# A hybrid attention and recurrence layer: merge-gate projections change places between two stages, and a hand-written timetable is redrawn

## The chip, the core and the metric

The kernel runs on one core of one Trainium2 chip. The metric is device time in microseconds (us) of one execution. The core's engines are PE (TensorE, matrix multiplication into PSUM banks), DVE (VectorE), ACT (ScalarE), POOL (GpSimd) and SP (SyncE, which issues the DMA transfers here). Each works through its own queue in order and waits for the others by semaphores.

## The reference

One decoder layer over 1024 tokens of width 1024. Two branches are computed from the same normalized input and merged by gates:

```python
xn = rms_norm(x, norm_g)
z = xn @ w_in                    # q, c_kv, q_idx, k_idx, w_idx, g_attn, x_rnn, g_rnn, merge
o = sparse_mla_attention(...)    # 16 heads; each query attends to the 256 keys with the best index scores
y_attn = (o * silu(g_attn)) @ w_attn_proj
h = rg_lru(causal_depthwise_conv(x_rnn, conv_w, conv_b), ...)   # gates r, i; a linear scan over time
y_rnn = (h * silu(g_rnn)) @ w_rnn_proj
gates = sigmoid(merge + b_merge)
g_a, g_r = gates[..., :1024], gates[..., 1024:]
return x + (g_a * y_attn + g_r * y_rnn) @ w_out       # and a final rms_norm
```

So there are two sets of merge gates: g_a (in the kernel "ma", for attention) and g_r ("mr", for the recurrence). Both are projections of the normalized input, and neither is needed before its branch's result.

## The kernel before

All activations are held transposed, channels on the 128 partitions and 1024 tokens along the free axis, so each projection of width 1024 is 8 tiles of 128 channels. A value is split into a high and a low fp32r part, and a product takes three matmuls (hi x hi, hi x lo, lo x hi). One projection tile is two halves of 512 tokens, 8 k-steps each, 48 matmuls (`proj_steps`, L115). Its weights come by DMA in two halves (`load_w`, L105): ACT makes the high part, POOL subtracts to get the low part (`split`, L93 to L95). The pool of weight parts holds two tiles, so weights are fetched one tile ahead.

The stages in order:

1. Normalization, the indexer's scores and two ma tiles (0 and 1) beside them.
2. The recurrence stage, written as a timetable: `at_time(t, fn, ...)` (L449) puts calls on a list `plan` with a time in planned us; the list is sorted and run (L822), and that order is then kept on PE, ACT, DVE and POOL (L821). SP's order is left to the scheduler. Planned times only order the work; each engine starts an instruction as soon as its inputs are there.
   - `long(t, kind, c)` (L515) places one projection tile in 16 steps of 0.68. Kinds: "xr" (recurrence input), "gr" (its SiLU gate), "ma", "mr", "rp" (recurrence output projection, which reads the recurrence's result u). A list `amid` of gate parts can be placed between the steps.
   - Four pairs of channel tiles. In each: one filling tile (ma), two xr, two gr. `conv` (L551) convolves on DVE; `both_parts` (L559) splits the result in two halves (ACT and POOL, tiles xs); `gate_part` (L567) makes the recurrence's gates on PE; `tail` (L743) places decay, root and scan of the pair one pair later; `scan` (L602) writes u to DRAM (u_r).
   - Beside this the threshold search for the 256 best keys, bit by bit, 31 rounds: `near_round` (L665) for four blocks of queries on DVE, `far_round` (L674) for the two longest on ACT with a small step on DVE.
   - The tail of the stage (from L783): another ma, eight mr and eight rp tiles on PE. `reload` (L738) fetches u from DRAM into two buffers in turn and splits it for rp. When a search ends, `needs` (L707) and `select` (L715) write each block's mask of distances `sd`; the last addition of `select` is on POOL (L728). `evac_rp` (L507) multiplies y_rnn by the gate mr on DVE and stores it (mr_d).
3. Attention: a planner (`step`, `work`, L1116 to L1154) puts projections for the next pair of heads (q, k, v, g) between the logits, transposes and outputs of the present pair; only PE's order is fixed. `left`, L1157, and L1165 put one merge tile, ma7, beside head pair 6. `merge` (L876) computes it and stores it (ga_d). `gated` (L1012) multiplies a finished pair's o by its gate and stores it.
4. Output projections of attention, merging, the final projection, normalization.

Of the kernel before, what the change touches and what calls it, by code (L numbers as in the profile page):

```python
# [8 lines left out]
F32 = mybir.dt.float32  # L9
# [43 lines left out]
def hybrid_kernel(ctx: ExitStack, tc: tile.TileContext, x, w_b, w_a, w_ap, w_rp, w_o, vecs,  # L53
# [36 lines left out]
    ga_d = [tc.dram_tile([P, S], F32, name=f"ga_d{c}") for c in range(8)]  # L90
    mr_d = [tc.dram_tile([P, S], F32, name=f"mr_d{c}") for c in range(8)]
# [59 lines left out]
    with ExitStack() as p12:  # L151
# [317 lines left out]
        def weights_of(kind, c):  # L469
            src = w_rp[c] if kind == "rp" else w_b[{"xr": G_XR, "gr": G_GR, "ma": G_MA, "mr": G_MR}[kind] + c]  # L470
            W[kind, c] = load_w(src, f"{kind}{c}")
# [20 lines left out]
        def evac_ma(n):  # L492
            g = (here["rn"] if "rn" in here else later["kp2"]).tile([P, S], F32, tag="ga", name=f"ga{n}", bufs=1)

            def evac(c0, m, acc):
                nc.scalar.activation(g[:, c0:c0 + m], acc, AF.Tanh, scale=0.5, bias=hbm[:, n:n + 1])
                nc.sync.dma_start(ga_d[n][:, c0:c0 + m], g[:, c0:c0 + m])
            return evac

        def evac_mr(n):  # L500
            g = gr[n] = grp.tile([P, S], F32, tag="gr", name=f"grm{n}")

            def evac(c0, m, acc):
                nc.scalar.activation(g[:, c0:c0 + m], acc, AF.Sigmoid, bias=col(V_BM + 8, n))
            return evac

# [8 lines left out]
        def long(t, kind, c, amid=(), first=5):  # L515
# [4 lines left out]
            evac = {"xr": evac_xr, "gr": evac_gr, "ma": evac_ma, "mr": evac_mr, "rp": evac_rp}[kind]  # L520
# [194 lines left out]
        def select(b):  # L715
# [12 lines left out]
            nc.gpsimd.tensor_tensor(out=sd[:, off(b):off(b + 1)], in0=s, in1=eq, op=ALU.add)  # L728
# [9 lines left out]
        def reload(c):  # L738
            raw = later["kp2"].tile([P, S], F32, tag=("eq", "pre")[c % 2], name=f"ur{c}")
            nc.sync.dma_start(raw, u_r[c])  # L740
            split(later["uh"][:, c], later["ul"][:, c], raw, nc.gpsimd if c % 3 == 2 else nc.vector)

        def tail(t, c, d):  # L743
            at_time(t + 2.0, decay, c)
            at_time(t + 5.4, radicand, c)
            at_time(t + 6.2, decay, d)
            at_time(t + 12.2, radicand, d)
            at_time(t + 12.3, root, c)
            at_time(t + 12.4, root, d)
            at_time(t + 14.0, scan, c)  # L750
            at_time(t + 20.4, scan, d)
# [3 lines left out]
        t, fill_in = 0.0, iter(range(2, 8))  # L755
        for p in range(4):
            c, d = 2 * p, 2 * p + 1
            t0 = t
            if p:
                tail(t0, c - 2, c - 1)  # L760
                near_round(t0 + 0.8)
                near_round(t0 + 7.0)
            else:
                for u in range(4):
                    near_round(t0 + 3.0 + 5.2 * u)
            at_time(t0 + 1.0, gate_weights, c)
            at_time(t0 + 12.5, gate_weights, d)
# [12 lines left out]
            t = long(t3, "gr", d, gate_parts(d), 3)  # L780
# [9 lines left out]
        at_time(t0 + 27.5, close_rec)  # L790
        at_time(t0 + 27.6, distances)
        near_round(t0 + 27.0)
        for c in range(8):
            at_time(t0 + 32.0 + 1.5 * c, reload, c)
# [618 lines left out]
```

## Time and profile before

| | us |
|---|---|
| median of 3 runs | 1252.97 (1252.04 to 1254.42) |
| the profiled execution | 1251.78 |
| its span, first to last instruction | 1249.9 |
| PE busy in the span | 1160.5 |
| DVE busy | 836.5 |
| ACT busy | 753.1 |
| POOL busy | 472.6 |
| mean granted TensorE clock | 0.967 |

In the profile a matmul's end is modelled and consecutive matmuls overlap, so a busy PE isn't a PE at its peak: the step from one matmul to the next tells more. The granted clock shows when PE was slowed. A line of a group gives the line in the code, the engine, the operation, what it writes and reads, the count, busy time, the mean in ns, and the idle time before it with what ended it. A line of the waits says who waited for whom: us in total, times, longest.

### The profile page before, as it was taken

To read this page: it belongs to the slowest core of one execution; us is meant where nothing else is said; L and a number is where in the kernel's file an instruction comes from. 1 tells how busy PE (TensorE), PEld (TensorE's weight loads), DVE (VectorE), ACT (ScalarE), POOL (GpSimd) and SP (SyncE) were. 2 spreads that over 40 slices of the span, in tenths; PEclk is the share of its full clock that TensorE was granted. 3 is DMA by queue.
4 is the path that set the end of the run, shared out by engine and by line. 5 is a ranking of instruction groups with operands and counts; after the bars stand their busy time and mean duration, and the time that the engine had idled before them with its cause. 6 is when DMAs were issued, how large, how long until landed. Compare 5 with 4: busy or idle time off the path is not lost.

```text
span 1249.9 us, 16199 instructions
## 1 busy us (share of the span) xinstructions
PE 1160.5 (93%) x5528; PEld 964.1 (77%) x5528; DVE 836.5 (67%) x1740; ACT 753.1 (60%) x1444; POOL 472.6 (38%) x385
## 2 busy tenths in 40 slices
PE   6989989999999989969999998988998999999997
PEld 5978868777777768848888776777877877788886
DVE  6887596868696677860387868776867598542335
ACT  6467459696969877311477766666667677332211
POOL 4211135455455322332344352525343526275000
PEclk8989999999999979979999998989999999999999
DMA  5111111222122422112200010110010232264322
GB/s 205 42 34 49 46 55 64 97 72 81 64 83 63 156 87 76 59 51 91 74 12 26 29 34 32 41 33 29 16 38 26 74 112 85 90 202 147 110 85 110
DMA packets 42674, 89.99 MB, mean 72 GB/s; under 512 B 5088, under 2 KB 8672, under 8 KB 42592
## 3 DMA queue, kind: packets, MB, share of 16 engines
q1 hardware_dynamic: 42448, 88.70, 21.2%
q8 instruction: 44, 0.72, 0.2%
q14 instruction: 38, 0.31, 0.1%
q10 hardware_dynamic: 144, 0.26, 0.1%
HBM read 68.49 MB, written 20.45 MB: 71 GB/s over the span
## 4 chain that ended last, share of the span: by engine, by line
PE 64%; DVE 20%; ACT 9%; issue 3%; POOL 1%; DMA 1%; SPq 0%; ACTq 0%; DVEq 0%; POOLq 0%
PE pT L1248 4%; DVE junk L631 3%; PE o L1202 2%; PE z_q L121 2%; PE z_q L122 2%; DVE xc L557 2%; PE f L113 2%; PE f L112 2%; PE f L111 2%; PE z_q L123 2%; PE l L1044 2%; PE l L1045 2%; PE z_ma L122 2%; PE z_ma L123 2%; PE z_ma L121 2%
## 5 line engine op out<-in xcount | busy, mean ns | idle before, releaser
L1251 ACT ACTIVATE pp<-pT 128x512 fp32r<-128x512 f32 (+1 forms) x160 | 87.8, 550 | 55.4 <-PE pT L1248 53.8
L1252 DVE TENSOR_TENSOR pp<-pT,pp 128x512 fp32r<-128x512 f32 (+1 forms) x160 | 100.7, 632 | 28.4 <-ACT pp L1251 26.7
L631 DVE TENSOR_SCALAR_CACHE_REDUCE junk<-sc,thr 128x384 bf16<-128x384 f32 (+4 forms) x130 | 106.3, 817 | 3.5
L1202 PE MATMUL o<-pp,vt 128*128 128x512 f32 x160 | 70.9, 443 | 17.2 <-DVE o L1217 13.8
L654 ACT ACTIVATE junk<-sc,neg 128x896 int8<-128x896 f32 (+1 forms) x62 | 67.8, 1093 | 17.7 <-DVE neg L661 16.6
L1052 ACT ACTIVATE l<-l,m 128x128 f32<-128x128 f32 (+4 forms) x80 | 54.3, 678 | 28.9 <-DVE m L1046 27.7
L1044 PE MATMUL l<-kh,qt 128*128 128x128 f32 (+2 forms) x192 | 66.5, 350 | 2.6 <-DVE m L1046 2.4
L1045 PE MATMUL l<-kl,qt 128*128 128x128 f32 (+2 forms) x192 | 66.9, 349 | 0.0
L121 PE MATMUL z_q<-xh,whi_q 128*128 128x512 f32 x128 | 55.4, 433 | 10.2 <-DVE kl L928 10.2
L123 PE MATMUL z_mr<-xh,wlo_mr 128*128 128x512 f32 x128 | 51.0, 398 | 11.4 <-POOL wlo_mr L95 11.4
L1046 DVE CUSTOM_DVE_ANT_0 l<-sc,l 128x512 f32<-128x512 f16 (+3 forms) x80 | 41.6, 523 | 26.8 <-PE l L1045 24.5
L1052 ACT ACTIVATE sc<-sc,m 128x384 f32<-128x384 f32 (+2 forms) x48 | 44.9, 935 | 23.4 <-DVE m L1046 22.2
L1217 DVE TENSOR_TENSOR o<-o,o 64x256 f32<-64x256 f32 x128 | 52.8, 418 | 8.9 <-ACT o L1215 6.5
L122 PE MATMUL z_rp<-url,whi_rp 128*128 128x512 f32 x128 | 52.4, 410 | 3.3 <-DVE url L95 1.7
L121 PE MATMUL z_rp<-urh,whi_rp 128*128 128x512 f32 x128 | 52.4, 409 | 3.2 <-ACT urh L94 3.1
L95 POOL TENSOR_TENSOR xs<-xc,xs 64x1024 fp32r<-64x1024 f32 x16 | 38.2, 2389 | 43.8 <-ACT xs L94 28.5
L377 ACT ACTIVATE r<-s 128x512 f32<-128x512 f32 (+1 forms) x80 | 39.8, 522 | 25.0 <-PE s L376 22.1
L1248 PE MATMUL pT<-ident,sc 128*128 128x128 f32 x288 | 50.0, 278 | 2.9 <-DVE pp L1252 2.9
L382 DVE SCALAR_TENSOR_TENSOR sc<-r,wi,sc 128x384 f32<-128x384 f32 (+5 forms) x42 | 40.6, 999 | 18.0 <-ACT r L377 17.7
L1057 POOL TENSOR_SCALAR sc<-sc,m 128x384 f32<-128x384 f32 (+1 forms) x32 | 25.6, 801 | 70.5 <-DVE m L1054 57.2
L123 PE MATMUL z_rp<-urh,wlo_rp 128*128 128x512 f32 x128 | 51.9, 405 | 0.0
L1248 PE MATMUL pT<-ident,l 128*128 128x128 f32 x288 | 49.6, 276 | 2.1 <-DVE m L1054 2.1
(358 smaller groups left out, 3928.0 us busy)
## 6 DMA issues: line engine op xcount, KB each, us to landing
xt<-in_x_dram SPq DMA_DIRECT2D x8, 512.0 KB, 8.9
wraw_xr<-in_w_b_dram SPq DMA_DIRECT2D x16, 256.0 KB, 2.7
wraw_gr<-in_w_b_dram SPq DMA_DIRECT2D x16, 256.0 KB, 2.9
u_r<-ig SPq DMA_DIRECT2D x8, 512.0 KB, 2.6
ur<-u_r SPq DMA_DIRECT2D x8, 512.0 KB, 3.3
wraw_mr<-in_w_b_dram SPq DMA_DIRECT2D x16, 256.0 KB, 2.8
wraw_rp<-in_w_rp_dram SPq DMA_DIRECT2D x16, 256.0 KB, 2.9
mr_d<-grm SPq DMA_DIRECT2D x16, 256.0 KB, 2.0
```

The source lines that it names most:

```text
L121: nc.tensor.matmul(acc, wh, xh_, start=(k == 0), stop=False)
L122: nc.tensor.matmul(acc, wh, xl_, start=False, stop=False)
L123: nc.tensor.matmul(acc, wl, xh_, start=False, stop=(k == KT - 1))
L631: nc.vector.tensor_scalar(junk[:, :P * (b + 1)], SL(b), thr_, None, op0=op, op1=ALU.add, accum_out=cnt[:, b - B0:b - B0 + 1])
L654: nc.scalar.activation(junk2[:, :P * (b + 1)], SL(b), AF.Sign, bias=nf[:, j:j + 1], accum_out=sums[:, j:j + 1])
L1044: nc.tensor.matmul(acc[:, :n], q, kh[:, c0:c0 + n], start=True, stop=False)
L1045: nc.tensor.matmul(acc[:, :n], q, kl[:, c0:c0 + n], start=False, stop=True)
L1052: nc.scalar.activation(l[:, :L], l[:, :L], AF.Exp, scale=-1.0, bias=mi, accum_out=m[:, 2:3])
L1202: nc.tensor.matmul(ov, vt[:, 2 * jj, :], pp[:, :, 0:256], start=(jj == 0), stop=False)
L1248: nc.tensor.transpose(tp[:, k * P:(k + 1) * P], pr[u][:, j * P:(j + 1) * P], ident)
L1251: latest[:] = [nc.scalar.activation(pp[:, 0, :n], tp[:, :n], AF.Copy), nc.vector.tensor_tensor(out=pp[:, 1, :n], in0=tp[:, :n], in1=pp[:, ...
L1252: nc.vector.tensor_tensor(out=pp[:, 1, :n], in0=tp[:, :n], in1=pp[:, 0, :n].bitcast(F32), op=ALU.subtract)]
```

## The change

The filling tile of each recurrence pair becomes an mr tile (mr0 to mr3 instead of ma2 to ma5). Their gates are stored to DRAM (gm_d) and fetched again (`again`) when rp has freed buffers; the tail keeps mr4 to mr7 and then runs rp in the order 4 to 7, 0 to 3. The ma tiles 2 to 7 all go to attention, one beside each of the head pairs 1 to 6. u is fetched at once, eight transfers straight into the tile of the low part, and split in place. The addition at the end of `select` gets a place of its own on the timetable. The places of convolutions, decays, roots, scans and search rounds change.

```diff
         def evac_mr(n):
-            g = gr[n] = grp.tile([P, S], F32, tag="gr", name=f"grm{n}")
+            if "rn" in here and n < 4:
+                g = T("g", n, bufs=1)
+            else:
+                g = gr[n] = grp.tile([P, S], F32, tag="gr", name=f"grm{n}")
 
             def evac(c0, m, acc):
                 nc.scalar.activation(g[:, c0:c0 + m], acc, AF.Sigmoid, bias=col(V_BM + 8, n))
+                if n not in gr:
+                    nc.sync.dma_start(gm_d[n][:, c0:c0 + m], g[:, c0:c0 + m])
             return evac
+
+        def again(n):
+            g = gr[n] = grp.tile([P, S], F32, tag="gr", name=f"grm{n}")
+            nc.sync.dma_start(g, gm_d[n])
...
-            nc.gpsimd.tensor_tensor(out=sd[:, off(b):off(b + 1)], in0=s, in1=eq, op=ALU.add)
+            later["sum", b] = lambda: nc.gpsimd.tensor_tensor(out=sd[:, off(b):off(b + 1)], in0=s, in1=eq, op=ALU.add)
+
+        def select_at(t, b):
+            at_time(t, select, b)
+            t += 0.0066 * P * (b + 1) + 0.7
+            at_time(t, lambda: later["sum", b]())
+            return t
...
-        def reload(c):
-            raw = later["kp2"].tile([P, S], F32, tag=("eq", "pre")[c % 2], name=f"ur{c}")
-            nc.sync.dma_start(raw, u_r[c])
-            split(later["uh"][:, c], later["ul"][:, c], raw, nc.gpsimd if c % 3 == 2 else nc.vector)
+        def fetch_u(c):
+            nc.sync.dma_start(later["ul"][:, c].bitcast(F32), u_r[c])
+
+        def part_u(c):
+
+            split(later["uh"][:, c], later["ul"][:, c], later["ul"][:, c].bitcast(F32),
+                  nc.gpsimd if c % 3 == 2 else nc.vector)
 
         def tail(t, c, d):
-            at_time(t + 2.0, decay, c)
-            at_time(t + 5.4, radicand, c)
-            at_time(t + 6.2, decay, d)
-            at_time(t + 12.2, radicand, d)
-            at_time(t + 12.3, root, c)
-            at_time(t + 12.4, root, d)
-            at_time(t + 14.0, scan, c)
-            at_time(t + 20.4, scan, d)
+            for u in (c, d):
+                at_time(t + 2.0, decay, u)
+                at_time(t + 5.36, radicand, u)
+                at_time(t + 5.4, root, u)
+            at_time(t + 12.4, scan, c)
+            at_time(t + 17.5, scan, d)
...
             if p:
                 tail(t0, c - 2, c - 1)
                 near_round(t0 + 0.8)
-                near_round(t0 + 7.0)
-            else:
-                for u in range(4):
-                    near_round(t0 + 3.0 + 5.2 * u)
+                far_round(t0 + 15.0)
...
-            t = long(t, "ma", next(fill_in))
-            far_round(t + 6.1)
-            far_round(t + 12.9)
+            t = long(t, "mr", p)
             t1 = long(t, "xr", c)
             t2 = long(t1, "xr", d)
-            at_time(max(t1 + 1.0, t0 + 26.0), conv, c)
-            at_time(max(t1 + 6.4, t0 + 31.4), both_parts, c)
-            near_round(t0 + 31.5)
-            at_time(t2 + 3.4, conv, d)
-            at_time(t2 + 8.7, both_parts, d)
-            near_round(t2 + 8.8)
-            t3 = long(t2, "gr", c, gate_parts(c))
-            t = long(t3, "gr", d, gate_parts(d), 3)
+            at_time(t1 + 0.8, conv, c)
+            at_time(t1 + 6.0, both_parts, c)
+            near_round(t1 + 6.1)
+            far_round(t1 + 2.4)
+            at_time(t2 + 0.8, conv, d)
+            at_time(t2 + 6.0, both_parts, d)
+            near_round(t2 + 6.1)
+            t3 = long(t2, "gr", c, gate_parts(c), 4)
+            near_round(t3 - 1.4)
+            t = long(t3, "gr", d, gate_parts(d), 4)
+            near_round(t - 7.5)
             far_round(t - 3.4)
 
         t0 = t
         tail(t0, 6, 7)
         near_round(t0 + 0.8)
-        near_round(t0 + 7.0)
-        t = long(t, "ma", next(fill_in))
-        for n in range(3):
+        for n in range(4, 8):
             t = long(t, "mr", n)
...
-            at_time(t0 + 32.0 + 1.5 * c, reload, c)
-        for n in range(8):
+            at_time(t0 + 24.0, fetch_u, c)
+            at_time(t0 + 28.7 + 2.5 * c, part_u, c)
+        for n in (4, 5, 6, 7, 0, 1, 2, 3):
             t = long(t, "rp", n)
-            if n + 3 < 8:
-                t = long(t, "mr", n + 3)
-        u = t0 + 17.0
+            if n > 3:
+                at_time(t + 1.0, again, n - 4)
+        u = t0 + 15.0
         while bits["far"] >= 0:
             far_round(u)
-            u += 5.0
+            u += 4.7
         far_end = u
-        u = t0 + 45.0
+        u = t0 + 23.2
         while bits["near"] >= 0:
-            u = max(near_round(u), u + 5.6)
-        at_time(u, nearest)
+            u = max(near_round(u), u + 5.0)
+        at_time(t0 + 60.0, nearest)
         at_time(u, needs, near, 0, n1)
         u += 4.0
         for b in near:
-            at_time(u, select, b)
-            u += 0.0075 * P * (b + 1)
+            u = select_at(u, b)
         u = max(u, far_end)
         at_time(u, far_last)
         at_time(u + 4.0, needs, FAR_B, n1, nb)
+        u += 7.0
         for b in FAR_B:
-            at_time(u + 7.0, select, b)
+            u = select_at(u, b)
...
-            left = [7]
+            left = list(range(2, 8))
...
-                m = [(i, []) for i in both("m", left.pop(0))] if hp == 6 else []
+                m = [(i, []) for i in both("m", left.pop(0))] if 0 < hp < 7 else []
```

More of the change, by code (lines that the diff above doesn't have):

```diff
@@ L90, in hybrid_kernel @@
     ga_d = [tc.dram_tile([P, S], F32, name=f"ga_d{c}") for c in range(8)]
+    gm_d = [tc.dram_tile([P, S], F32, name=f"gm_d{c}") for c in range(4)]
     mr_d = [tc.dram_tile([P, S], F32, name=f"mr_d{c}") for c in range(8)]
@@ L469, in weights_of @@
         def weights_of(kind, c):
-            src = w_rp[c] if kind == "rp" else w_b[{"xr": G_XR, "gr": G_GR, "ma": G_MA, "mr": G_MR}[kind] + c]
+            src = w_rp[c] if kind == "rp" else w_b[{"xr": G_XR, "gr": G_GR, "mr": G_MR}[kind] + c]
             W[kind, c] = load_w(src, f"{kind}{c}")
@@ L490, in evac_gr @@
             return evac
[L492 to L498, printed above, removed]
         def evac_mr(n):
-            g = gr[n] = grp.tile([P, S], F32, tag="gr", name=f"grm{n}")
+            if "rn" in here and n < 4:
+                g = T("g", n, bufs=1)
+            else:
+                g = gr[n] = grp.tile([P, S], F32, tag="gr", name=f"grm{n}")
             def evac(c0, m, acc):
                 nc.scalar.activation(g[:, c0:c0 + m], acc, AF.Sigmoid, bias=col(V_BM + 8, n))
-            return evac
+                if n not in gr:
+                    nc.sync.dma_start(gm_d[n][:, c0:c0 + m], g[:, c0:c0 + m])
+            return evac
+        def again(n):
+            g = gr[n] = grp.tile([P, S], F32, tag="gr", name=f"grm{n}")
+            nc.sync.dma_start(g, gm_d[n])
         def evac_rp(n):
@@ L519, in long @@
             at_time(begin[order[-2]] + 0.3 if len(order) > 1 else t - LONG, weights_of, kind, c)
-            evac = {"xr": evac_xr, "gr": evac_gr, "ma": evac_ma, "mr": evac_mr, "rp": evac_rp}[kind]
+            evac = {"xr": evac_xr, "gr": evac_gr, "mr": evac_mr, "rp": evac_rp}[kind]
             rhs = (lambda k: (later["uh"][:, k], later["ul"][:, k])) if kind == "rp" else xhl
@@ L736, in close_rec @@
             later["ul"] = urp.tile([P, KT, S], F32R, name="url")
-        def reload(c):
-            raw = later["kp2"].tile([P, S], F32, tag=("eq", "pre")[c % 2], name=f"ur{c}")
-            nc.sync.dma_start(raw, u_r[c])
-            split(later["uh"][:, c], later["ul"][:, c], raw, nc.gpsimd if c % 3 == 2 else nc.vector)
-        def tail(t, c, d):
-            at_time(t + 2.0, decay, c)
-            at_time(t + 5.4, radicand, c)
-            at_time(t + 6.2, decay, d)
-            at_time(t + 12.2, radicand, d)
-            at_time(t + 12.3, root, c)
-            at_time(t + 12.4, root, d)
-            at_time(t + 14.0, scan, c)
-            at_time(t + 20.4, scan, d)
+        def fetch_u(c):
[3 more added lines that the diff above has]
+                  nc.gpsimd if c % 3 == 2 else nc.vector)
+        def tail(t, c, d):
+            for u in (c, d):
[4 more added lines that the diff above has]
+            at_time(t + 17.5, scan, d)
         at_time(-LONG - 1, open_rec)
         at_time(-5.0, signs)
-        t, fill_in = 0.0, iter(range(2, 8))
+        t = 0.0
         for p in range(4):
@@ L785, in hybrid_kernel @@
         near_round(t0 + 0.8)
-        near_round(t0 + 7.0)
-        t = long(t, "ma", next(fill_in))
-        for n in range(3):
+        for n in range(4, 8):
             t = long(t, "mr", n)
-        at_time(t0 + 27.5, close_rec)
-        at_time(t0 + 27.6, distances)
-        near_round(t0 + 27.0)
+        at_time(t0 + 23.0, close_rec)
+        at_time(t0 + 23.1, distances)
         for c in range(8):
-            at_time(t0 + 32.0 + 1.5 * c, reload, c)
-        for n in range(8):
+            at_time(t0 + 24.0, fetch_u, c)
+            at_time(t0 + 28.7 + 2.5 * c, part_u, c)
+        for n in (4, 5, 6, 7, 0, 1, 2, 3):
             t = long(t, "rp", n)
-            if n + 3 < 8:
-                t = long(t, "mr", n + 3)
-        u = t0 + 17.0
+            if n > 3:
+                at_time(t + 1.0, again, n - 4)
+        u = t0 + 15.0
         while bits["far"] >= 0:
             far_round(u)
-            u += 5.0
+            u += 4.7
         far_end = u
-        u = t0 + 45.0
+        u = t0 + 23.2
         while bits["near"] >= 0:
-            u = max(near_round(u), u + 5.6)
-        at_time(u, nearest)
+            u = max(near_round(u), u + 5.0)
+        at_time(t0 + 60.0, nearest)
         at_time(u, needs, near, 0, n1)
```

## The prediction

> **What bounds the kernel now.** I read the page first, then busy time by stage (columns: window, length, then busy us and instruction count of PE, PEld, DVE, ACT and POOL, the granted clock, DMA share, GB/s), then PE's waits inside the two stages that the change touches.
>
> ```profile
> PE 1160.5 (93%) x5528; PEld 964.1 (77%) x5528; DVE 836.5 (67%) x1740; ACT 753.1 (60%) x1444; POOL 472.6 (38%) x385
> ```
> ```profile
> 141.00:389.30 248.30, 236.45 (x1030) 192.85 (x1029) 191.31 (x281) 182.98 (x289) 125.79 (x84) 0.99 0.22 72
> 389.30:432.80 43.50, 43.50 (x193) 36.04 (x192) 29.46 (x46) 36.83 (x63) 15.10 (x12) 1.00 0.37 125
> 432.80:555.00 122.20, 106.23 (x435) 83.16 (x433) 93.42 (x183) 64.97 (x138) 32.97 (x25) 0.92 0.21 69
> 555.00:603.60 48.60, 46.71 (x191) 37.51 (x192) 3.44 (x5) 7.60 (x14) 15.79 (x14) 0.93 0.29 94
> 603.60:618.70 15.10, 15.10 (x80) 12.97 (x78) 7.83 (x13) 8.82 (x17) 6.95 (x7) 1.00 0.20 66
> 618.70:1077.80 459.10, 423.73 (x2207) 352.13 (x2206) 346.33 (x916) 325.67 (x677) 192.61 (x172) 0.96 0.13 42
> ```
> ```profile
> PE rg L573 <- POOL xs L95: 11.9, 7, 5.7
> PE z_mr L123 <- POOL wlo_mr L95: 11.4, 1, 11.4
> ...
> PE o L1202 <- DVE o L1217: 13.8, 8, 3.9
> PE z_q L121 <- DVE kl L928: 10.2, 3, 4.1
> ```
>
> The windows are: the four recurrence pairs (141.0 to 389.3), the tail behind them (389.3 to 603.6, in three pieces), the opening of attention up to its first logits (618.7), attention's loop, and (not shown) the final projection from 1077.8. PE is the bound in the pairs and the tail, with a few named waits (the first two rows of waits lie there, the last two in attention). DVE is nearly done by 555.0: in the tail's last 48.6 us it works 3.44 us. In attention nobody is full: PE's 423.73 of 459.1 counts overlapping matmuls, and its waits are for short chains through DVE.
>
> **The change, part by part.** All starts here are in us from the span's start.
>
> ```profile
> 267.60 0.39 PE L121 MATMUL z_ma<-xh,whi_ma 128*128 128x512 f32 x1
> ...
> 328.46 0.39 PE L121 MATMUL z_ma<-xh,whi_ma 128*128 128x512 f32 x1
> ...
> 339.34 0.39 PE L121 MATMUL z_xr<-xh,whi_xr 128*128 128x512 f32 x1
> ```
>
> A projection tile (48 matmuls) takes 339.34 - 328.46 = 10.9 us of PE. Five of them (ma2 to ma6) leave this stage for attention: 54.4 us that must be paid there unless it fills idle time.
>
> *The pairs.* The tile count stays (mr0 to mr3 stand where ma2 to ma5 stood; Sigmoid replaces Tanh on the same 128x512 shape, which I cost at nothing, since ACT has 65 us free in this window). A pair takes 328.46 - 267.60 = 60.9 us. What can go is the wait for the input halves xs. The first pair lost 5.7 us because four threshold rounds stood ahead of its convolution on DVE; they move behind it. In the later pairs the convolution starts 2.6 to 3.4 us earlier, and the second tile's gate parts come two steps later. In exchange ACT meets the second tile's xs copy earlier and stands some 3 us until the first tile's last gate part frees the buffer; behind it wait only evacuations, for which PE has six banks. So I take the 11.9 us and about 1 us of reduced clock: gain 13, bounds -3 (a far_step placed ahead of a convolution waits for ACT) to 14. Tail start: 389.3 - 13 = 376.3.
>
> The new stores of mr0 to mr3 and their reloads add 8 transfers of 256 KB and 4 of 512 KB; the ma stores of the same size leave.
>
> ```profile
> ur<-u_r SPq DMA_DIRECT2D x8, 512.0 KB, 3.3
> ...
> mr_d<-grm SPq DMA_DIRECT2D x16, 256.0 KB, 2.0
> ```
>
> A reload takes about 3.3 us and is issued four tiles, 43 us, before its use, after the buffer's mr_d store (2.0 us) has gone out. On SP's queue it stands ahead of weights that are due a tile later. Cost nothing; without that cover, 3.3 us each.
>
> *The tail on PE.* It falls from 17 tiles to 12: 12 x 10.9 = 130.8 us instead of 214.3. The 11.4 us wait for wlo_mr also goes: POOL stood in select's last addition, waiting for DVE, with the weights' subtraction queued behind; that addition now has its own, later place. The reload of u is issued at 24 us into the tail, all eight at once into place; the last part is due at 46.2, while rp's first half reaches its k=7 at 48. Eight transfers of 3.3 us one after another from 27 would end at 53, so PE may stand up to 7 us there. On SP the eight fetches first wait for the recurrence's last u_r store, and rp's first weights (issued at 33, due at 43.5) queue behind them.
>
> *The tail on DVE decides.* It must do the same work in the shorter stage, and three rounds more.
>
> ```profile
> 457.94 0.60 DVE L631 TENSOR_SCALAR_CACHE_REDUCE junk<-sc,thr 128x384 bf16<-128x384 f32 x1
> ...
> 461.76 0.61 DVE L631 TENSOR_SCALAR_CACHE_REDUCE junk<-sc,thr 128x384 bf16<-128x384 f32 x1
> ```
> ```profile
> L723 DVE TENSOR_SCALAR eq<-sc,thr 128x384 f32<-128x384 f32 (+5 forms) x6 | 4.5, 751 | 5.8 <-POOL sc L728 5.8
> ```
>
> Its busy time in the tail is 29.46 + 93.42 + 3.44 = 126.3. The pairs now hold 15 of the 31 near rounds instead of 18, so the tail has 16 instead of 13: three more at 461.76 - 457.94 = 3.82, 11.5. The waits of select for POOL stay: 5.8. At the head of the tail (decays, roots, two scans) DVE was idle 43.5 - 29.46 = 14 us; the roots come earlier now, and I keep 7 (bounds 0 and 14). For far steps that wait for ACT while it does the eight u halves, and for POOL's extra density, I add 5 (0 to 15). Sum 155.6 us. So selection ends 25 us after PE's last rp tile, and PE's slack makes the 7 us stand at rp free.
>
> *The hand-over.* PE's opening takes 15.1 us (the row 603.60:618.70), so PE would be ready for logits 130.8 + 15.1 = 145.9 us into the tail. DVE is ready after 155.6, and 163.4 if all 7.83 us of that row stand behind the selection. The first blocks' logits don't need the last masks, so some overlap; I take 160 (bounds 146 and 175). Before it was 618.7 - 389.3 = 229.4. Gain 69.4 (54 to 83). PE then stands some 14 us, and comes out of it slow:
>
> ```profile
> 756.34 0.77 PE L1202 MATMUL o<-pp,vt 128*128 128x512 f32 x1 [3.94 <-DVE o L1217]
> ```
> ```profile
> 753.40:760.20 6.80, 3.86 (x12) 3.11 (x12) 4.40 (x12) 2.60 (x7) 0.58 (x1) 0.50 0.01 2
> ```
>
> After a wait of 3.94 us the clock is 0.50 for a window of 6.8 us and the matmul takes 0.77 us. I charge 3.4 us, half such a window. The Trainium skill ("TensorE: Matmul & The Clock Gate", Part 1) says that an idle window of about 3.4 us halves the clock and a busy one restores it; the trace agrees, and by that rule the charge would be about half, an estimate of 1.7.
>
> *Attention* takes five more merge tiles, one each beside pairs 1 to 5 (pair 6 had one already). The pair boundaries and three pairs as windows:
>
> ```profile
> 746.59 2.39 POOL L1015 TENSOR_TENSOR o<-o,sga 128x1024 f32<-128x1024 f32 x1
> ...
> 985.93 2.39 POOL L1015 TENSOR_TENSOR o<-o,sga 128x1024 f32<-128x1024 f32 x1 [1.55 <-DVE o L1217]
> ```
> ```profile
> 863.30:920.40 57.10, 51.74 (x266) 43.12 (x265) 44.14 (x114) 39.70 (x85) 24.31 (x23) 0.94 0.09 30
> 920.40:985.30 64.90, 59.23 (x305) 49.47 (x304) 43.19 (x114) 44.62 (x92) 29.00 (x26) 0.95 0.11 34
> 985.30:1034.20 48.90, 46.72 (x251) 38.60 (x250) 40.56 (x114) 36.14 (x77) 15.28 (x15) 1.00 0.36 119
> ```
> ```profile
> 995.25 0.47 PE L1202 MATMUL o<-pp,vt 128*128 128x512 f32 x1 [0.62 <-ACT pp L1251]
> ```
>
> Pair 4 (first window) has no merge tile: 266 matmuls in 57.1 us, 0.215 each, clock 0.94. Pair 6 has one running across its start: 251 in 48.9 us, 0.195 each, clock 1.00. The difference is the wait ten us after a pair's start, where PE needs a bank that waits for o, the gate on POOL (2.39) and a store: 3.94 us in pair 2 (with the slow window), 0.62 us in pair 6, where merge matmuls fill the time. At pair 6's pace a pair 4 with 48 matmuls more takes 314 x 0.195 = 61.2, 4.1 more; at pair 5's pace (64.9 / 305 = 0.213) 66.8, 9.7 more; with nothing filled 10.9. I take 7, five times: 35 (bounds 20 and 54.5). DVE's 44.14 of 57.1 leaves room, the q wait on kl (10.2) is untouched. The merge evacuations share two buffers with q's; q follows two tiles, 22 us, later, against a store of 2.0.
>
> *The sum* against the profiled execution (1251.78; span 1249.9, 1.9 around it): -13 - 69.4 + 3.4 + 35 = -44.0, so 1207.8. The median of the runs, 1252.97, is 1.2 higher: **1209.0**.
>
> **The rivals.**
> *Attention pays in full.* The waits are chains of fixed length and only move: 54.5 instead of 35, 1209.0 + 19.5 = 1228.5. For it: the loop's waits are latencies. Against: the 0.62 us in pair 6.
> *DVE's tail is no bound.* Attention's work slips between the selections and the head of the tail has no idle: logits 146 us into the tail without a clock loss, and attention at 20: 1209.0 - 14 - 3.4 - 15 = 1176.6. Against it: the sum of 155.6.
> *Slower: POOL blocks DVE in the tail.*
>
> ```profile
> 515.75 2.77 POOL L95 TENSOR_TENSOR wlo_mr<-wraw_mr,whi_mr 128x512 fp32r<-128x512 f32 x2
> ...
> 517.42 2.46 DVE L724 TENSOR_TENSOR_SCAN pre<-ones,eq 128x640 f32<-128x640 f32 x1
> ```
> ```profile
> 524.52 1.76 DVE L724 TENSOR_TENSOR_SCAN pre<-ones,eq 128x768 f32<-128x768 f32 x1
> ```
>
> A scan of 640 beside POOL's subtraction takes 2.46 us, a scan of 768 alone 1.76. The tail's POOL work, 15.10 + 32.97 + 15.79 = 63.9 us, now lies wholly beside a DVE queue without gaps. If every microsecond of it held DVE, logits would come at 224 and the time would be 1209.0 + 63.9 = 1272.9; the kernel is slower once about 44 us are held, 70% of it. For it: these rows. Against it: the 126.3 us already contain such holds, and the counts, most of DVE's work, show none (0.60 and 0.61). The Trainium skill ("SBUF — State Buffer", "SBUF: two separate sides") states that the two engines share a port pair as an exclusive lock for a whole instruction, if DVE's operation has two SBUF inputs or a 2-port mode. The rows of the scan agree with it.
> *The change does nothing on balance*: the selection ends late (175), the pairs gain nothing and attention pays in full: 1209.0 + 15 + 13 + 19.5 = 1256.5.
>
> **How the numbers follow.** The forecast 0.55 (its own range 1190 to 1222); attention in full 0.20; DVE no bound 0.12; POOL's hold 0.07 (0.04 slower, 0.01 same, 0.02 faster); nothing on balance 0.06 (a third each). Same means within 0.2%, about what a measurement of this kernel tells from no change. The range 1186 to 1238 takes in attention in full and a late hand-over on the one side, half of the second rival on the other; about 2 in 10 lie outside. Faster 0.91, same 0.03, slower 0.06.
>
> **What would show it.** Right: no wait of rg for xs or of z_mr for wlo_mr; rp's last matmul some 131 to 138 us after the tail's start near 376, DVE busy nearly throughout and its last selection (L727) near 532; first logit near 536 behind a PE gap of about 14 us; attention's pairs 1 to 5 at 62 to 68 us with the waits for L1217 small. Wrong: PE dense into the first logits (DVE is not the bound), pairs that are 11 us longer with their waits kept, L643 and the scans stretched in the tail, or rp waiting for urh over 20 us.

## The result and the profile after

| | before | after |
|---|---|---|
| median, us (4 runs each, same chip) | 1252.51 (1248.61 to 1254.42) | 1200.34 (1199.21 to 1200.73) |
| the profiled execution | 1251.78 | 1199.21 |
| its span | 1249.9 | 1197.0 |

The ratio is 0.9586, with a 95% interval of 0.9562 to 0.961. The forecast was 1209.0. In the code of after the lines stand one to six further down: L121 is L122, L507 is L513, L728 is L730, L928 is L933, L1217 is L1222.

The busy time by engine from the page of after: PE is busy 14 us less in a span that is 53 us shorter; DVE, ACT and POOL are within 11 us of what they were.

```profile
PE 1146.1 (96%) x5528; PEld 954.7 (80%) x5528; DVE 843.5 (70%) x1740; ACT 752.7 (63%) x1444; POOL 483.6 (40%) x385
```

Busy time by stage of before, for two stretches that the prediction did not cut in this way (window, length, busy us and count of PE, PEld, DVE, ACT, POOL, granted clock, DMA share, GB/s): the pairs from the first xr matmul on, and all of attention from its first logit to the first matmul of the final projection.

```profile
152.00:389.30 237.30, 225.45 (x977) 183.74 (x977) 185.83 (x273) 178.77 (x281) 123.71 (x78) 0.99 0.22 71
618.70:1155.00 536.30, 500.93 (x2548) 416.03 (x2547) 369.37 (x943) 346.52 (x707) 235.56 (x198) 0.97 0.18 61
```

The same view of after: the pairs, the tail in four pieces (four mr tiles; the first rp tile; the other seven rp tiles; the opening of attention), attention, and the final stage.

```profile
152.00:379.30 227.30, 224.08 (x978) 182.60 (x977) 198.61 (x270) 174.78 (x270) 129.21 (x77) 1.00 0.22 72
...
379.30:424.10 44.80, 43.65 (x194) 35.82 (x192) 33.78 (x57) 37.32 (x64) 12.56 (x9) 1.00 0.43 153
424.10:457.20 33.10, 19.89 (x49) 11.92 (x50) 21.14 (x55) 23.61 (x48) 10.53 (x7) 0.59 0.12 40
457.20:535.60 78.40, 78.40 (x338) 63.17 (x337) 63.51 (x122) 40.99 (x94) 30.31 (x24) 1.00 0.36 120
535.60:556.30 20.70, 16.85 (x80) 14.15 (x79) 15.12 (x18) 9.13 (x18) 10.62 (x8) 0.92 0.19 61
556.30:1102.20 545.90, 540.68 (x2788) 452.84 (x2787) 363.37 (x944) 357.28 (x727) 246.71 (x208) 1.00 0.21 69
1102.20:1197.00 94.80, 87.48 (x409) 73.24 (x407) 38.79 (x85) 20.25 (x51) 4.79 (x2) 0.98 0.29 100
```

Read down the lengths. The pairs fell by 237.3 - 227.3 = 10.0. From the tail's start to the first logit it was 618.7 - 389.3 = 229.4 and is 556.3 - 379.3 = 177.0: 52.4 less. Attention rose from 536.3 to 545.9: 9.6. The final stage is unchanged (94.9 and 94.8). Together -52.9, the difference of the spans. The row that stands out is the second of the tail: 48 matmuls, 10.9 us of work, took 33.1 us at a clock of 0.59.

PE's waits in the tail of after (us in total, times, longest):

```profile
PE z_rp L122 <- ACT urh L95: 7.4, 2, 4.2
PE k L112 <- DVE grm L513: 3.8, 1, 3.8
PE z_rp L123 <- DVE url L96: 3.1, 3, 2.1
PE z_rp L123 <- POOL url L96: 2.0, 2, 1.5
```

The wait for wlo_mr (11.4 before) is gone. In the pairs these waits of rg are left:

```profile
PE rg L575 <- POOL ig L582: 1.7, 3, 0.6
PE rg L575 <- POOL xs L96: 1.4, 2, 0.7
```

Longer are the waits of the first rp tile for the halves of u. In the kernel before they were these, and the tile took 23.7 us (432.8 to 456.5):

```profile
PE z_rp L121 <- ACT urh L94: 3.1, 2, 1.8
PE z_rp L122 <- DVE url L95: 1.7, 3, 0.8
PE z_rp L122 <- POOL url L95: 1.6, 1, 1.6
```

How they come about in after can be read from the timeline of after around 444 us (start, duration, engine, line, operation, idle before and what ended it):

```profile
435.11 1.22 DVE L96 TENSOR_TENSOR url<-url,urh 128x1024 fp32r<-128x1024 f32 x1 [3.44 <-ACT urh L95]
...
439.30 0.15 DVE L663 TENSOR_TENSOR neg<-neg,flip 128x2 int32<-128x2 int32 x1
...
439.49 1.04 ACT L656 ACTIVATE junk<-sc,neg 128x896 int8<-128x896 f32 x1 [3.46 <-DVE neg L663]
...
442.97 1.04 ACT L95 ACTIVATE urh<-url 128x1024 fp32r<-128x1024 f32 x1
...
444.05 1.22 DVE L96 TENSOR_TENSOR url<-url,urh 128x1024 fp32r<-128x1024 f32 x1 [4.02 <-ACT urh L95]
...
444.07 0.79 PE L122 MATMUL z_rp<-urh,whi_rp 128*128 128x512 f32 x1 [4.24 <-ACT urh L95]
...
449.44 1.04 ACT L656 ACTIVATE junk<-sc,neg 128x896 int8<-128x896 f32 x1 [3.44 <-DVE neg L663]
```

ACT has the far search's sums and the copies of u in one queue; DVE has the near search's counts, the far search's small step (neg) and the low parts of u in one queue. ACT stood 3.46 us until neg came; neg stood on DVE behind a low part that had waited 3.44 us for a copy, and behind the near counts that follow it. Then ACT did its sums, while the next copy waited behind them; DVE stood 4.02 us for that copy, with the near counts and the next neg behind it. Neither engine is full in this stretch (DVE 21.14 of 33.1 us, ACT 23.61), each waits for the other in turn, and PE waits for both.

### The profile page after: what moved, and what is told of

It reads as the page before. It is cut to its first block, busy times and chain, and to the rows that moved or that the text cites. A ratio compares the mean times of both kernels' runs of the same rounds, so it can differ in the third digit from the quotient of the medians.

```text
span 1197.0 us, 16205 instructions
## 1 busy us (share of the span) xinstructions
PE 1146.1 (96%) x5528; PEld 954.7 (80%) x5528; DVE 843.5 (70%) x1740; ACT 752.7 (63%) x1444; POOL 483.6 (40%) x385
## 4 chain that ended last, share of the span: by engine, by line
PE 68%; DVE 13%; ACT 12%; issue 3%; DMA 2%; POOL 1%; SPq 0%; POOLq 0%; ACTq 0%; DVEq 0%
PE pT L1253 5%; PE o L1207 3%; PE l L1049 3%; PE l L1050 3%; DVE xc L559 2%; PE z_rp L123 2%; PE f L112 2%; PE f L113 2%; PE f L114 2%; PE z_rp L124 2%; PE z_rp L122 2%; PE z_q L122 2%; PE z_q L123 2%; PE z_q L124 2%; PE z_g L122 2%
## 5 line engine op out<-in xcount | busy, mean ns | idle before, releaser
L1207 PE MATMUL o<-pp,vt 128*128 128x512 f32 x160 | 67.0, 419 | 1.2 <-DVE m L1059 0.7
L122 PE MATMUL z_rp<-urh,whi_rp 128*128 128x512 f32 x128 | 53.2, 416 | 8.5 <-ACT urh L95 7.4
L1222 DVE TENSOR_TENSOR o<-o,o 64x256 f32<-64x256 f32 x128 | 53.4, 419 | 6.8 <-ACT o L1220 4.6
L122 PE MATMUL z_q<-xh,whi_q 128*128 128x512 f32 x128 | 53.1, 415 | 0.2 <-DVE kl L933 0.2
L1057 ACT ACTIVATE sc<-sc,m 128x384 f32<-128x384 f32 (+2 forms) x48 | 44.9, 935 | 12.7 <-DVE m L1051 11.4
L1059 DVE RECIPROCAL m<-m 128x1 f32<-128x1 f32 x128 | 20.4, 159 | 43.2 <-ACT l L1057 23.8
L124 PE MATMUL z_q<-xh,wlo_q 128*128 128x512 f32 x128 | 50.2, 392 | 0.0
L123 PE MATMUL z_q<-xl,whi_q 128*128 128x512 f32 x128 | 50.2, 392 | 0.0
```

The costliest lines, as they stand in the source:

```text
L122: nc.tensor.matmul(acc, wh, xh_, start=(k == 0), stop=False)
L123: nc.tensor.matmul(acc, wh, xl_, start=False, stop=False)
L124: nc.tensor.matmul(acc, wl, xh_, start=False, stop=(k == KT - 1))
L1057: nc.scalar.activation(l[:, :L], l[:, :L], AF.Exp, scale=-1.0, bias=mi, accum_out=m[:, 2:3])
L1207: nc.tensor.matmul(ov, vt[:, 2 * jj, :], pp[:, :, 0:256], start=(jj == 0), stop=False)
```

## The experiments

Where no other number is given, a run's time is the median of four, the ratio is to the kernel before in the same job, and starts and ends come from its profiled execution.

**What a merge tile costs in attention.** Three runs. First, the kernel before with the five merge tiles computed once more in attention (the first stages stay as they were):

```
-            left = [7]
+            left = list(range(2, 8))
-                m = [...] if hp == 6 else []
+                m = [...] if 0 < hp < 7 else []
```

> The kernel before, with the merge tiles ma2 to ma6 computed a second time beside head pairs 1 to 5, as the changed kernel does in attention; its recurrence stage stays as it was. In the two traces the stretch from the first logit to the final projection is 536.3 us before and 545.9 us after. Theory F (the tiles fill waits: a pair's first merge tile removes the waits for o and kl and the half-clock windows behind them): 2 us per tile, so 1262 us, and PE's waits for L1217 and L928 fall from 24 us to below 3. Theory of the prediction, 7 us per tile: 1288. Rival R (full price of 10.9 us per tile; attention became shorter for another reason, the state in which it starts): 1307.

1262.89 us, ratio 1.0083 (1.0068 to 1.0098): 10.8 more than the kernel before in the same job (1252.08). Attention's window and its waits for o and kl:

```profile
620.20:1165.90 545.70, 539.43 (x2788) 451.61 (x2787) 363.96 (x943) 357.31 (x727) 248.01 (x208) 1.00 0.21 69
```
```profile
PE o L1202 <- DVE o L1217: 1.0, 1, 1.0
```

240 matmuls more (2788 against 2548), 54.4 us of PE work, made the stage 545.7 - 536.3 = 9.4 us longer. The wait for o fell from 13.8 to 1.0, the wait for kl from 10.2 to 0.2, and the clock went from 0.97 to 1.00. Theory F, that the tiles fill idle time, stands.

Second, the other way round: the changed kernel without ma2 to ma6 (L1162 and L1170 as before; the merge reads ma7's gate in their place).

> The changed kernel without the merge tiles ma2 to ma6 (it leaves those five gate tiles out and reads ma7's in their place). Theory F: the waits and half-clock windows come back, so only about 10 us are saved: 1190. At 7 us per tile: 1165. Rival R: all 54 us are saved, 1146.

1192.82 us, ratio 0.9517 (0.9501 to 0.9533): 7.5 less than after. The old waits are back:

```profile
558.50:1096.60 538.10, 502.55 (x2548) 417.35 (x2548) 371.33 (x944) 346.81 (x707) 235.09 (x198) 0.97 0.18 61
```
```profile
PE o L1207 <- DVE o L1222: 14.9, 9, 3.9
PE z_q L122 <- DVE kl L933: 10.0, 3, 4.0
```

Third, the same tiles, two beside each of pairs 2, 4 and 6 and none beside 1, 3 and 5:

```
-                m = [(i, []) for i in both("m", left.pop(0))] if 0 < hp < 7 else []
+                m = [(i, []) for _ in range(2) for i in both("m", left.pop(0))] if hp in (2, 4, 6) else []
```

> The changed kernel with the same six merge tiles, two beside each of head pairs 2, 4 and 6 and none beside 1, 3 and 5. Theory F: a pair without a tile takes 57 to 61 us again and a pair with two about 72, so 20 to 27 us more than the changed kernel: 1220 to 1227. Rival R (PE's work alone counts, and it is the same): 1200.

1221.51 us, ratio 0.9751 (0.9731 to 0.9771): 21 more than after, with the same work. Its window and the wait that came back:

```profile
556.30:1123.90 567.60, 547.22 (x2787) 454.92 (x2787) 366.81 (x944) 357.96 (x727) 248.70 (x208) 0.99 0.20 67
```
```profile
PE z_q L122 <- DVE kl L933: 8.0, 3, 3.4
PE o L1207 <- DVE o L1222: 0.5, 2, 0.2
```

The time is inside theory F's 1220 to 1227, but only the wait for kl came back; the wait for o stayed away. Nor did the pairs come out at 57 to 61 and 72 us: from one pair's gating on POOL to the next it took 62 to 69 us in each of the first five stretches, since the matmuls of two tiles reach beyond their pair. So the price of a tile is taken from the totals. The first in a pair costs 7.5 / 5 to 10.8 / 5, 1.5 to 2.2 us. Taking three first tiles away saves about 5.5 by that, yet the time grew by 21, so a second tile in the same pair cost about 26.5 / 3 = 9 us of its 10.9, an estimate.

**The reload in place.** The changed kernel with the old reload through two buffers, at the new times of the parts:

```
...
-            at_time(t0 + 24.0, fetch_u, c)
-            at_time(t0 + 28.7 + 2.5 * c, part_u, c)
+            at_time(t0 + 28.7 + 2.5 * c, reload, c)
```

> The changed kernel with u fetched as before, into two buffers in turn, at the new places of the splits. In the changed kernel the first rp tile stands some 25 us, most of it behind ACT's copies of u, which stand between rounds of the far search. Theory A (ACT's order sets this stand): the fetch hardly matters, 1200 to 1204. Rival D (the transfers set it, as each would now wait for the split before the last): 10 to 15 us more, 1210 to 1215.

1200.54 us, ratio 0.9588 (0.9572 to 0.9604): no difference to after. The first rp tile ends at 457.6 instead of 457.2. The fetch in place was worth nothing: in after the last of the eight transfers had landed by 422.7 (issued at 412.1, and the longest of the eight took 10.6), and ACT copied the last part at 444.96, so the parts wait in the queues and not for the data.

**What makes the first rp tile stand.** Two runs leave out five rounds of one search each, at the time of that tile:

```
-            far_round(u)
+            if t0 + 26.0 < u < t0 + 50.0:
+                bits["far"] -= 1
+            else:
+                far_round(u)
```

> The changed kernel without the five rounds of the far search whose place is 29 to 48 us into the tail (five bits of two thresholds are left out). Theory A (the far search sets the tail: each round needs 3 us of ACT, waits for its step in DVE's queue, and holds up ACT's copies of u): the first rp tile stands under 10 us instead of 25, the last selection ends 25 us or more earlier, the first logit comes 18 to 25 us earlier: 1175 to 1183. Rival D (DVE's queue sets it, as the prediction had it): only five steps of 0.2 us go, 1197 to 1200.

1194.96 us, ratio 0.9532 (0.9518 to 0.9546). Neither expectation held. The same edit on the near rounds:

> The changed kernel without the five rounds of the near search whose place is 28 to 48 us into the tail (five bits of four thresholds are left out). Rival D: 5 x 3.8 us of DVE go, the first logit comes 15 to 19 us earlier: 1181 to 1186. Theory A: ACT's far rounds still stand between the copies of u; they wait less for DVE, so some of the gain, at most 8 us: 1192 to 1199.

1196.87 us, ratio 0.9549 (0.9533 to 0.9565): inside the first theory's 1192 to 1199, far from the other's 1181 to 1186. Each search alone was worth little: the first rp tile ended 4.3 and 2.0 us earlier. So I asked whether the one keeps the stand that the other would free, and left out both:

> The changed kernel without five rounds of the far search and five rounds of the near search, those that stand 26 to 50 us into the tail (the two searches then fix five bits fewer each). Without the five far rounds alone the first rp tile ended 4.3 us earlier, without the five near rounds alone 2.0 us earlier. Theory S, the two queues hold each other (ACT's copies of u stand behind far sums that wait for DVE, DVE's subtractions stand behind near counts and behind a far step that waits for ACT), so either search alone keeps most of the stand and only both together free it: the first rp tile ends at 438 to 446 instead of 457, the first logit 99 us later at 537 to 545, the time is 1181 to 1189. Theory T, the two searches cost the rp tile separately, 4.3 + 2.0 us, and the rest of the stand comes from something else (the fetch, the weights): the first rp tile ends at 450 to 452, the first logit at 549 to 551, 1192 to 1195.

1185.18 us, ratio 0.9456 (0.9442 to 0.947): inside theory S's 1181 to 1189. The first rp tile ended at 442.9, 14.3 us earlier, against 4.3 + 2.0 = 6.3 for the two alone. Its windows (mr tiles; first rp tile; the other seven; opening of attention):

```profile
379.50:424.10 44.60, 43.67 (x194) 35.85 (x192) 30.56 (x47) 34.54 (x57) 12.56 (x9) 1.00 0.42 154
424.10:442.90 18.80, 14.11 (x49) 9.96 (x50) 11.76 (x9) 11.89 (x19) 14.93 (x7) 0.82 0.24 70
442.90:521.30 78.40, 78.40 (x338) 62.83 (x337) 63.48 (x121) 41.08 (x93) 28.75 (x23) 1.00 0.36 120
521.30:542.60 21.30, 17.02 (x80) 14.23 (x79) 15.64 (x19) 9.12 (x18) 10.94 (x8) 0.92 0.17 59
```

Beside after's four rows only the second has changed much: 18.8 instead of 33.1. The third is 78.4 in both, the last 21.3 and 20.7. Milestones of all runs on this stage, in us from the span's start, read from their traces:

| run | first rp tile ends | last far step | last selection ends | first logit | logit behind rp tile | median |
|---|---|---|---|---|---|---|
| after | 457.2 | 517.1 | 541.8 | 556.3 | 99.1 | 1200.34 |
| far_less | 452.9 | 512.8 | 537.6 | 552.1 | 99.2 | 1194.96 |
| near_less | 455.2 | 515.1 | 539.8 | 554.4 | 99.2 | 1196.87 |
| both_less | 442.9 | 502.8 | 527.9 | 542.6 | 99.7 | 1185.18 |
| far_later | 450.9 | 528.9 | 551.8 | 563.3 | 112.4 | 1208.64 |
| lockstep | 450.3 | 528.5 | 552.0 | 565.0 | 114.7 | 1208.57 |
| far_ahead | 454.4 | 512.7 | 539.9 | 555.7 | 101.3 | 1196.95 |
| both_ahead | 450.3 | 510.2 | 535.2 | 550.4 | 100.1 | 1193.28 |
| evac_first | 456.7 | 516.6 | 543.6 | 556.5 | 99.8 | 1201.71 |

In the first four rows the list of work behind the stand is the same, and everything behind it moves with the stand's end: the first logit comes 99 us after it, wherever it is.

**Other timetables for the rounds.** If the stand is what costs, the rounds can be moved out of its way. Two attempts kept all rounds in the tail. far_later issues no far round between 24 and 47 us into the tail and the rest 4.0 apart:

```
-            u += 4.7
+            u += 4.7 if u < t0 + 24.0 else 4.0
+            if t0 + 24.0 < u < t0 + 47.0:
+                u = t0 + 47.0
```

> The changed kernel, nothing left out, with the far rounds kept away from ACT's copies of u: none begins between 24 and 47 us into the tail, then one each 4.0 us instead of 4.7. Theory A: the stand at the first rp tile falls from 25 to under 10 us, but the far search itself gets no shorter, so its end and the first logit move little: 1192 to 1204. Rival D: the stand is covered by DVE in any case: 1200, selection as late as before.

1208.64 us, ratio 0.9639 (0.9624 to 0.9653): 8 slower than after, which neither theory had. lockstep puts a far and a near round in step, 4.2 apart, with u's parts 1.9 apart in a pause of both:

```
-            at_time(t0 + 28.7 + 2.5 * c, part_u, c)
+            at_time(t0 + 31.0 + 1.9 * c, part_u, c)
...
+        T_ = 4.2
...
-            u += 4.7
+            u += T_
+            if t0 + 25.0 < u < t0 + 45.0:
+                u = t0 + 24.2 + 5 * T_ - 0.04
...
```

> As far_later, and the two searches in step: one far and one near round each 4.2 us, the far search's step on DVE placed right ahead of a near round, the copies of u 1.9 us apart. Theory A: a far round (3 us of ACT) now runs under a near round (3.8 us of DVE) with no wait on either side, so the far search ends some 20 us earlier and the first logit 12 to 20 us earlier: 1180 to 1188. Rival D: DVE's work is the same, 1198 to 1202.

1208.57 us, ratio 0.9641 (0.9627 to 0.9655): missed as well. The table shows why. Both shortened the stand by 6 to 7 us, and in both the far search ended 11 to 12 us later and the last selection 10 us later. One round depends on the one before it: sums on ACT, step on DVE, sums again. In after this round trip takes 5.9 us (517.1 - 405.5 = 111.6 us for 19 steps), waits included, so it is no lower bound: behind the pause far_later did 17 steps in 82.7 us, 4.9 each. That made up only part of the pause. Its fourth step of the tail came at 446.3, 28.9 us later than after's fourth, and its last one 11.8 us later; in lockstep the fifth step came 22.8 us later and the last one 11.4. In far_later PE then stood 11.6 us before the first logit. So the stage has two limits that lie close together, PE's stand and the end of the far search.

Then rounds must leave the tail altogether. far_ahead does five more far rounds in the pairs and pauses in the tail as far_later does:

```
             if p:
                 ...
                 near_round(t0 + 0.8)
-                far_round(t0 + 15.0)
+            far_round(t0 + 15.0)
...
             near_round(t2 + 6.1)
+            far_round(t2 + 2.4)
...
```

> The whole computation. The changed kernel with five more far rounds in the four pairs (one more in each, two more in the first), so that the tail holds 15 instead of 20; in the tail none is issued from 24 to 47 us into it, the rest follow 4.0 us apart. Theory S (PE's stand at the first rp tile and the end of the far search bind in turn; moving the rounds alone cost 8 us because the far search ended at 529): the first rp tile ends at 450 to 453, the far search ends before 513, the first logit comes 99 to 101 us after the first rp tile, at 550 to 554, the pairs are 0 to 2 us longer since ACT works 184 of their 249 us; 1193 to 1199. Rival: ACT's further rounds delay gate parts and conv parts in the pairs by 1 us and more each, PE waits for them, the tail starts 4 us later or more, and the time is 1200 to 1206.

1196.95 us, ratio 0.955 (0.9536 to 0.9565), inside theory S's time; the first rp tile ended later than it said, 454.4 instead of 450 to 453, and the first logit at 555.7 instead of 550 to 554. The tail started 1.2 us later than in after. both_ahead also does four near rounds more in the pairs, and in the tail leaves the slots at the first rp tile empty:

```
                 near_round(t0 + 0.8)
-                far_round(t0 + 15.0)
+                near_round(t0 + 6.6)
+            else:
+                near_round(t0 + 13.5)
+            far_round(t0 + 15.0)
...
-            far_round(u)
+            if not t0 + 26.0 < u < t0 + 50.0:
+                far_round(u)
             u += 4.7
...
```

> The whole computation. The changed kernel with five more far rounds and four more near rounds in the four pairs (two far rounds more in the first pair, one near round and one far round more in each), and in the tail none of the far rounds from 26 to 50 us and none of the near rounds from 26 to 45 us into it; the other rounds of the tail stand where they stood. Theory S (the two searches at the place of rp's first tile make the stand, and the rest of the list takes 99 us from its end): the tail goes as where ten rounds were left out, except for one near round; the first rp tile ends 64 to 67 us into the tail and the first logit comes 99 to 101 us later. The pairs: DVE works 209 of their 249 us and ACT 184; 24 us more on DVE and 15 to 20 us more on ACT fit, but in order they hold conv parts and gate parts up by at most a few us: the tail starts at 380 to 385, the first logit comes at 543 to 552, the time is 1186 to 1195. Rival: the pairs have no room for both searches, the rounds are worth on PE in the pairs what they were worth in the tail (14.6 us for ten), the tail starts at 390 or later: 1196 to 1202.

1193.28 us, ratio 0.9525 (0.951 to 0.9541): below after's interval, the fastest version of the whole computation here. In its windows the first rp tile takes 18.8 us, as with the rounds left out, and the pairs pay for it:

```profile
152.60:387.30 234.70, 225.18 (x977) 182.28 (x976) 212.96 (x315) 188.19 (x305) 129.70 (x77) 1.00 0.21 70
...
431.50:450.30 18.80, 13.68 (x48) 9.76 (x49) 15.21 (x19) 11.92 (x19) 14.97 (x7) 0.91 0.21 70
```

The pairs are 234.7 instead of 227.3, 7.4 more. I had expected the tail to start by 385; it started at 387.3. DVE works 213 of 235 us there, and PE's waits of rg for xs are 5.1 us instead of 1.4. Half of what the tail gained went back.

**The hand-over.** In after PE's k waited 3.8 us for a bank that two evictions on DVE free, and these stood behind the last selection. evac_first places that selection behind them:

```
         for b in FAR_B:
             u = select_at(u, b)
+            u = max(u, t + 3.0)
```

> The whole computation. The changed kernel with the selection of the last block placed behind the two evictions of the last rp tile on DVE, where it stood ahead of them. Theory H (PE's k waited 3.8 us for the bank that these evictions free, and all up to the first logit follows from k): k starts 3 to 4 us earlier, the first logit 2.5 to 4 us earlier at 552.5 to 554, 1196.5 to 1198. Rival: k comes earlier, but DVE's part of it, kl, now stands behind the selection, which ends near 545 instead of 542 while kl ran at 548; or the attention's first tile waits for the last block's distances from POOL: the first logit moves by under 1 us, 1199.5 to 1201.

1201.71 us, ratio 0.9589 (0.9573 to 0.9605): no gain. k came 4.5 us earlier, at 537.9, and the first logit at 556.5 instead of 556.3. The timeline of after, then of evac_first, shows what came last:

```profile
541.88 2.37 POOL L730 TENSOR_TENSOR sc<-sc,eq 128x1024 f16<-128x1024 f32 x1 [3.09 <-DVE sc L729]
...
542.45 0.80 PE L112 MATMUL k<-cnh,ukh 128*128 128x512 f32 x1 [3.85 <-DVE grm L513]
...
545.67 2.07 ACT L899 ACTIVATE vr<-v 128x512 f32<-128x512 f32 x4 [0.36 <-DMA mr_d<-grm]
```
```profile
543.72 2.39 POOL L730 TENSOR_TENSOR sc<-sc,eq 128x1024 f16<-128x1024 f32 x1 [1.82 <-DVE sc L729]
...
546.14 1.09 ACT L900 ACTIVATE vr<-v 128x512 f32<-128x512 f32 x2 [6.53 <-POOL sc L730]
...
556.45 0.45 PE L1050 MATMUL l<-kh,qt 128*128 128x128 f32 x1 [6.09 <-POOL wlo_g L96]
```

In after PE has no further wait between its k at 542.45 and the first logit at 556.26: the matmuls of k and of one tile of q fill these 13.8 us. In evac_first they were done at 550.2, and PE stood 6.09 us for other work. The row names the release that came last; the chain that the profile follows back from there leads over ACT's copies to POOL's addition.

The copies of v on ACT waited in evac_first for POOL's last addition of the selection, and the copies of k and q, with kl behind them, come after those in ACT's queue. In after they started at 545.67, when ACT had stood 5.93 us for PE's k and a store of a gated tile was out, so there the addition was no longer what they waited for. So the rival held, but by POOL's addition rather than by kl on DVE, and behind the wait that was removed stood a second one that ended at the same time. That the copies wait for memory of the earlier stage which attention's tiles take over is my reading of it; no run gave attention memory of its own.

## Why the prediction was right, and where it was not

The direction and the size came out (1209.0 forecast, 1200.34 measured), but the nearness of the figure is luck: errors of opposite sign cancelled. Against the sum's -44.0, the pairs gave 3.0 less, the tail 13.6 less, and attention cost 25.4 less, which makes -52.9 between the spans.

*The pairs, 13 forecast, 10.0 measured.* The first pair gave more than its 5.7: from its first gr tile to its second it took 193.9 - 173.8 = 20.1 us and takes 186.5 - 173.7 = 12.8. The other three gave 1.6, 0.6 and 0.5 (from one filling tile to the next) instead of 6.2 between them; waits of rg of 1.4 us for xs and 1.7 us for ig remain. The mechanism was right, the later pairs were overrated. No run changes the places in the pairs alone; that they gave the 10.0 is read from the waits.

*The tail on PE, 130.8 forecast, 156.3 measured* (379.3 to 535.6; 131 to 138 was named as a sign of being right). The 11.4 us wait for wlo_mr went, as said; no run gives select's addition its own place without the rest. Eleven of the twelve tiles cost what was said within 3.3 us (44.8 for four, 78.4 for seven, at 10.9 each). The other is the one at which I allowed "up to 7 us" for transfers of u and called them free. The stand was 33.1 - 10.9 = 22.2 us: 13.2 us of waits (0.71, 1.45, 3.12, 0.47, 0.58, 4.24, 0.47 and 2.14 in the timeline), and 9.0 for matmuls at half clock, at steps of 0.43 us instead of 0.23. This is the step that failed in kind, not in size. The transfers, landed by 422.7, were not what made it. The tail of before already had such a stand, 23.7 - 10.9 = 12.8 us; counting twelve tiles at 10.9 took it as gone, though the splits of u and both searches stayed. And I counted the stand as covered because DVE was to finish later than PE. But DVE and ACT stood in the same place: the circle of the timeline above. A stand that two engines share is not cover for either. both_less shows its worth: 14.3 us less stand, 13.7 us earlier logits.

*The tail on DVE, "decides", 155.6 to the end of the selection.* Measured: 541.8 - 379.3 = 162.5. The near rounds were miscounted: the pairs of after hold 19 (four in the first, five in each of the others), not 15, so the tail has one fewer than before and not three more, four times 3.82 = 15.3 us too much work. Against that, DVE stood idle 37.9 us and not 17.8. Its busy time up to the selection's end, and its waits in that window:

```profile
379.30:541.80 162.50, 124.56 (x237) 0.92 0.32 109
```
```profile
DVE neg L663 <- ACT flip L660: 13.5, 4, 4.7
DVE url L96 <- ACT urh L95: 10.1, 4, 4.0
DVE grm L513 <- PE z_rp L124: 5.6, 5, 2.3
DVE eq L725 <- POOL sc L730: 4.0, 3, 1.6
```

My 5 us for "far steps that wait for ACT" stand against 13.5 + 10.1. DVE's queue did set when PE's k could start, but as a partner in a chain, not as a full engine. The rival that "DVE's tail is no bound" was half right: there was idle time, but no logit came earlier for it. POOL held DVE little: 124.56 us busy for 126.3 minus one round is 2 us over.

*The hand-over, 160 forecast, 177.0 measured.* The selection ended 6.9 us later than forecast, and from there to the first logit it took 14.5 us where I had 4.4. I had assumed that "the first blocks' logits don't need the last masks, so some overlap". There was hardly any: PE's k waited for a bank that two evictions behind the selection free, and k and q take 13.8 us from there. With these evictions ahead (evac_first), attention's first copies stood behind the selection's last addition. PE's gap of 14 us behind a finished rp did not appear, since rp itself was late; 3.85 us before k were left, and the slow clock behind them cost 1.5 us (13.8 for k and q instead of evac_first's 12.3) where I had charged 3.4.

*Attention, +35 forecast, +9.6 measured.* The mis-sized term is the 7 us per tile. I had compared pairs 4, 5 and 6 of the kernel before and taken a value between them; "the q wait on kl (10.2) is untouched" was wrong, it fell to 0.2. The rows account for most of it: 54.4 us of tiles, minus 24 us of waits for o and kl, minus the slow clock (3% of 536, about 16 us), is 14; 9.4 (gates_twice against before) and 7.8 us (after against gates_left_out) were measured. PE's matmuls in the changed loop stand so close that the rival "attention pays in full" would have needed every one of those waits to survive; in two_by_two the wait for kl did, 8.0 us, and the time rose by 21.

*The new transfers at nothing.* Right: no wait of PE or of rp's evictions in the tail is for the reloaded gates, and the old way of reloading u gave the same time.

## What to carry to other kernels

Extra matmuls in a stretch with waits can cost far less than their time: here 1.5 to 2.2 us for the first 10.9-us tile of a head pair, which also kept the clock up, and, by the totals, about 9 us for a second one. So spread them, one to each gap. When two dependent chains share two in-order queues crosswise, neither busy sums nor slack of one engine tell the time: follow one full round trip through the queues, and ask of each stand who else stands in it.

## What the runs showed of the hardware

The clock fell without a wait as long as 3.4 us. Four windows of 3.4 us of after, around the start and the end of the slow stretch in the first rp tile (the columns as above; the clock is the third number from the end):

```profile
422.60:426.00 3.40, 1.53 (x6) 0.72 (x5) 3.29 (x11) 3.28 (x6) 1.82 (x2) 1.00 0.04 16
426.00:429.40 3.40, 1.95 (x6) 1.03 (x5) 1.66 (x4) 3.33 (x9) 3.04 (x2) 0.50 0.45 154
449.60:453.00 3.40, 3.40 (x9) 2.63 (x9) 3.33 (x8) 2.79 (x7) 0.00 (x0) 0.50 0.32 121
453.00:456.40 3.40, 3.40 (x15) 2.73 (x15) 1.98 (x9) 2.99 (x8) 0.00 (x0) 0.95 0.00 0
```

Behind a window in which PE was busy for 1.53 of 3.40 us the clock was 0.50, though its named waits there were 1.16 and 0.71 us; it came back behind a window that was busy throughout. The Trainium skill ("TensorE: Matmul & The Clock Gate", Part 1) puts half speed behind at least one idle window of about 3.4 us and full speed behind a busy one; the second half agrees with the trace, the first asks for more than the trace did: a window that was less than half busy did the same.

In the traces of all 14 kernels here the clock changes only at points that lie whole multiples of 3.41 us apart, so these windows can be counted. Behind each of the 59 windows at full clock in which PE was busy, by the profile's modelled times, for less than 40% the clock was 0.50; behind none of the 4575 above 60% it was, and behind 19 of the 37 between. From 0.50 it came back behind each of the 65 windows above 90%, behind 13 of the 20 at 80 to 90% and behind none of the 100 below. The slow stretch that the prediction showed is one of these cases: there the clock was 0.50 from 753.40 on, one us into the wait of 3.94 us that it was put down to, and this is the window ahead of it:

```profile
750.00:753.40 3.40, 1.25 (x8) 0.68 (x6) 3.40 (x9) 2.17 (x5) 3.10 (x3) 1.00 0.57 211
```
